# RMSNorm with swish on 16384 rows of 512: units of 8 rows instead of 4

## The chip, the core and the metric

The kernel runs on one core of a Trainium2 chip. A core has several engines that run side by side, each with its own queue of instructions: VectorE (DVE in the profile), ScalarE (ACT), GpSimd (POOL), SyncE (SP, which only issues transfers here) and TensorE (PE, which here only passes semaphores on). Sixteen DMA engines move data between the chip's memory (HBM) and the core's on-chip memory (SBUF). The metric is the device time of one execution in microseconds (us). Less is better.

## The reference

```python
x: (16, 1024, 512) float32, gamma: (512,) of ones, eps = 1e-5
rms = np.sqrt(np.mean(x ** 2, axis=-1, keepdims=True) + eps)
x_norm = x / rms * gamma
return (x_norm * (1.0 / (1.0 + np.exp(-x_norm)))).astype(np.float32)
```

The input is 33.55 MB and so is the output. Each element is read once and written once.

## The kernel before

The 16384 rows are spread over 128 partitions, 128 rows each, and "row" below means one row on each of the 128 partitions (2 KB each, 262 KB in all). A piece (a, n) is the rows a to a+n-1. All work is done in place in a ring `xb` of 96 rows in SBUF, so rows 96 to 127 take the places of rows 0 to 31 once these are stored.

SyncE's queue holds an order written out by hand (`order`). First come the loads of rows 0 to 95 in seven pieces. The queue then waits until (64,28) has landed, issues the stores (0,16) and (16,16), and then the loads (96,16), (112,12) and (124,4); the first of them waits for store (0,16), the second for store (16,16). It waits again until (112,12) has landed and issues the remaining stores (32,32), (64,32), (96,16), (112,8) and (120,8). Each store waits until `s_swish` has counted the units that cover its rows (`ends`). At the end the queue waits for the last stores.

Work goes in units of `cn` = 4 rows, 32 units in all. For unit k:

- `square` (ScalarE, L193 and L199): two rows are squared one at a time, with the hardware summing them into `ms` (each is an activation followed by a read of the accumulator); the two others are squared together into `sq`, which lies in the accumulator memory PSUM.
- `sums` (VectorE, L220): one reduction of `sq` gives the other two columns of `ms`.
- `power` (GpSimd, L175 and L182): adds eps, then raises to the power -0.5, giving `rstd`.
- `norm` (VectorE, L230): each row times its `rstd` times gamma, one instruction a row, in place.
- `swish` (ScalarE, L205): one Silu over the four rows, in place.

The engines are staggered by `lead` = 2 units. ScalarE goes: square of unit k+2, Silu of unit k. VectorE goes: sums of unit k+1, norm of unit k. ScalarE, VectorE and GpSimd each have a hardware loop with `turn` = 3 units per round, ten rounds. `ms`, `rstd` and `sq` have three buffers, one for each unit of a round. The place in the ring is computed in registers: ahead of nearly each instruction stands a register instruction that computes its address. TensorE's queue waits for each load in turn and counts the landed units into `s_land`, for which the squares wait.

Of the kernel before, what the change touches and what calls it, by code (L numbers as in the profile page):

```python
# [9 lines left out]
def kernel(  # L10
# [7 lines left out]
    nc = tc.nc  # L18
    P = nc.NUM_PARTITIONS
    AF = mybir.ActivationFunctionType  # L20
    ALU = mybir.AluOpType
    fp32 = mybir.dt.float32
# [3 lines left out]
    R, D = xf.shape  # L26

    groups = [16, 16, 32, 32, 16, 16]
    ring = 96
    loads = [(0, 4), (4, 4), (8, 8), (16, 16), (32, 32), (64, 28), (92, 4)]  # L30
    second = len(loads)
    loads += [(96, 16), (112, 12), (124, 4)]
    stores = [(0, 16), (16, 16)]
    storing = len(stores)
    stores += [(32, 32), (64, 32), (96, 16), (112, 8), (120, 8)]
    order = [("load", i) for i in range(second)]
    order += [("landed", loads.index((64, 28)))]
    order += [("store", t) for t in range(storing)]
# [1 line left out]
    order += [("landed", loads.index((112, 12)))]  # L40
    order += [("store", t) for t in range(storing, len(stores))]
    early = 2
    cn = 4
    n_sq = 2
    turn = 3
    lead = 2

    first = [sum(groups[:g]) for g in range(len(groups))]
# [9 lines left out]
    K = rows_each // cn  # L58
    assert (K - lead) % turn == 0 and ring % (turn * cn) == 0
    rounds = (K - lead) // turn  # L60
    per_ring = ring // (turn * cn)
# [9 lines left out]
    inv_d = 1.0 / float(D)  # L71
# [5 lines left out]
    def sbuf(name, shape, dt=fp32):  # L77
        return nc.alloc_sbuf_tensor(name, shape, dt).ap()

    xb = sbuf("xb", [P, ring, D])  # L80
    gamma4 = sbuf("gamma4", [P, D])
    gamma_sb = sbuf("gamma_sb", [P, D])
    neg_half = sbuf("neg_half", [P, cn])
# [1 line left out]
    aeps = sbuf("aeps", [P, turn, cn])  # L85
    rstd = sbuf("rstd", [P, turn, cn])
    sq = [nc.alloc_psum_tensor(f"sq{i}", [P, n_sq, D], fp32).ap() for i in range(turn)]
    junk = [nc.alloc_psum_tensor(f"junk{i}", [P, D], fp32).ap() for i in range(2)]
    junk += [sbuf(f"junk{i}", [P, D]) for i in range(2, turn * (cn - n_sq))]

    ld = [nc.alloc_semaphore(f"ld{t}") for t in range(len(loads))]
    st = [nc.alloc_semaphore(f"st{t}") for t in range(len(stores))]
# [2 lines left out]
    s_half = nc.alloc_semaphore("s_half")  # L95
    s_gamma = nc.alloc_semaphore("s_gamma")
    s_land = nc.alloc_semaphore("s_land")
    s_acc = nc.alloc_semaphore("s_acc")
    s_sq = nc.alloc_semaphore("s_sq")
    s_sum = nc.alloc_semaphore("s_sum")  # L100
    s_eps = nc.alloc_semaphore("s_eps")
    s_rstd = nc.alloc_semaphore("s_rstd")
# [3 lines left out]
    def need(ins, sem, value):  # L106
        return ins.wait_op(sem, value, "sem-ge")
# [17 lines left out]
    def load(i):  # L125
        a, n = loads[i]
        for u, (c, m) in enumerate(stores):
            over = c + ring < a + n and a < c + m + ring
            if over and u not in stored_by_sync:
                nc.sync.wait_ge(st[u], 16)  # L130
                stored_by_sync.add(u)
        return nc.sync.dma_start(
            out=buf(loads[i]), in_=dram(xf, loads[i])
        ).then_inc(ld[i], 16)
# [9 lines left out]
    for t in range(early):  # L144
        ins = load(t).ins
        assert here[-1] is ins or here[-1].name == ins.name
        here.pop()
        at = next(
            i for i, other in enumerate(entry)
            if other.engine == mybir.EngineType.SP  # L150
            and isinstance(other, mybir.InstDrain)
        )
# [7 lines left out]
    def take(queue, sem, n):  # L160
        need(queue.nop(nofuse=True), sem, n).then_inc(sem, -n)
# [10 lines left out]
    def power(k, nth):  # L172
        m = k % turn
        need(
            nc.gpsimd.tensor_scalar(  # L175
                out=aeps[:, m, :], in0=ms[:, m, :], scalar1=eps_f, scalar2=None,
                op0=ALU.add,
            ),
            s_sum, nth + 1,
        ).then_inc(s_eps, 1)  # L180
        need(
            nc.gpsimd.tensor_tensor(  # L182
                out=rstd[:, m, :], in0=aeps[:, m, :], in1=neg_half, op=ALU.pow
            ),
            s_eps, nth + 1,
        ).then_inc(s_rstd, 1)

    def rows(at, n):
        return xb[:, at : at + n, :] if isinstance(at, int) else xb[:, bass.ds(at, n), :]

    def square(k, at, sem, count, accs):
        for j in range(n_sq, cn):
            acc = nc.scalar.activation(  # L193
                out=junk[(k % turn) * (cn - n_sq) + j - n_sq], in_=rows(at + j, 1)[:, 0, :], func=AF.Square,
                scale=inv_d**0.5, accum_out=ms[:, k % turn, j : j + 1],
            )
            if j == n_sq:
                need(acc, sem, count)
        nc.scalar.activation(  # L199
            out=sq[k % turn], in_=rows(at, n_sq), func=AF.Square, scale=inv_d**0.5,  # L200
        ).then_inc(s_sq, 1)

    def swish(at, nth):
        need(
            nc.scalar.activation(out=rows(at, cn), in_=rows(at, cn), func=AF.Silu),  # L205
            s_norm, nth + 1,
        ).then_inc(s_swish, 1)
# [5 lines left out]
    nc.scalar.preload_act_table_set("silu_and_others")  # L213
    for k in range(lead):
        assert landings[k] == [k]
        square(k, k * cn, ld[k], 16, k * (cn - n_sq))

    def sums(k, nth):
        need(
            nc.vector.tensor_reduce(  # L220
                out=ms[:, k % turn, 0:n_sq], in_=sq[k % turn], op=ALU.add,
                axis=mybir.AxisListType.X,
            ),
            s_sq, nth + 1,
        ).then_inc(s_sum, 1)

    def norm(k, at, nth):
        for j in range(cn):
            row = rows(at + j, 1)[:, 0, :]
            ins = nc.vector.scalar_tensor_tensor(  # L230
                out=row, in0=row, scalar=rstd[:, k % turn, j : j + 1], in1=gamma_sb,
                op0=ALU.mult, op1=ALU.mult,
            )
            if j == 0:
                need(ins, s_rstd, nth + 1)
        ins.then_inc(s_norm, 1)

    sums(0, 0)
    need(
# [1 line left out]
    ).then_inc(s_gamma, 1)  # L241
    nc.vector.wait_ge(s_gamma, 1)

    with nc.Fori(0, rounds, engines=[mybir.EngineType.Activation]) as i:  # L244
        now = nc.scalar.snap((i % per_ring) * (turn * cn))
        then = nc.scalar.snap(((i + 1) % per_ring) * (turn * cn))
        for m in range(turn):
            behind = now + (m + lead) * cn if m + lead < turn else then + (m + lead - turn) * cn
            square(m + lead, behind, s_land, m + 1, lead * (cn - n_sq) + m * (cn - n_sq))
            swish(now + m * cn, m)  # L250
        take(nc.scalar, s_land, turn)
        take(nc.scalar, s_norm, turn)
    for m in range(lead):
        swish((rounds * turn + m) * cn % ring, m)

    with nc.Fori(0, rounds, engines=[mybir.EngineType.DVE]) as i:
        now = nc.vector.snap((i % per_ring) * (turn * cn))
        for m in range(turn):
            sums(m + 1, m + 1)
            norm(m, now + m * cn, m)  # L260
        take(nc.vector, s_sq, turn)
        take(nc.vector, s_rstd, turn)
    sums(K - 1, 1)
    for m in range(lead):
        norm(rounds * turn + m, (rounds * turn + m) * cn % ring, m)

    with nc.Fori(0, rounds, engines=[mybir.EngineType.Pool]) as i:
        for m in range(turn):
            power(m, m)
        take(nc.gpsimd, s_sum, turn)  # L270
        take(nc.gpsimd, s_eps, turn)
    for m in range(lead):
        power(rounds * turn + m, m)

    for t in range(len(stores)):
        if t not in stored_by_sync:
# [36 lines left out]
```

## Time and profile before

| | |
|---|---|
| time, median of 3 runs (range) | 159.81 us (159.76 to 160.4) |
| profiled execution, its own time | 159.97 us |
| its span, first to last instruction | 158.5 us |
| ScalarE busy | 129.7 us (82% of the span) |
| VectorE busy | 124.5 us (79%) |
| GpSimd busy | 65.4 us (41%) |
| moved | 67.12 MB, 424 GB/s over the span |
| norm, one row of 512 (L230) | 744 ns |
| Silu, 4 rows (L205) | 1903 ns |
| reduction, 2 rows (L220) | 1224 ns |
| square, 2 rows together (L199) | 1005 ns |
| square, 1 row (L193) and the read of its sum | 603 ns and 186 ns |
| add of eps and power, 4 columns (L175, L182) | 643 ns and 1378 ns |

How to read the lines that follow. A page line of groups gives line, engine, operation, output and input, count, busy time and mean length. A line of waits gives who waited for whom, the total, the number of times and the longest. A line of the timeline gives start, length, engine, line and operation; in brackets stands the idle time ahead of it and what ended it. A name with a q (SPq, PEq) is the engine's own queue. The DMA row of the page gives the busy share of the DMA engines in 40 equal slices of the span, in tenths, where 9 is 90% or more.

### The profile page before, as it was taken

How to read it: one execution, taken by the hardware profiler on the slowest of the kernel's cores; microseconds unless marked ns; L12 is line 12 of the kernel's file. 1: busy time of each engine (PE TensorE's matmuls, PEld its weight loads, DVE VectorE, ACT ScalarE, POOL GpSimd, SP SyncE). 2: the span in 40 equal slices, each digit the busy share in tenths (PEclk: the TensorE clock that was granted, in tenths of full speed). 3: DMA queues.
4: the chain of work that ended last, by engine and by line, in shares of the span. 5: the costliest groups of instructions: out<-in, count | busy, mean ns of one | idle time of the engine just before them, and what ended most of it. 6: DMA issues, size and time to landing. Idle time of an engine off the chain costs nothing. (4 is left out here: it accounts for less than half of the span.)

```text
span 158.5 us, 896 instructions
## 1 busy us (share of the span) xinstructions
DVE 124.5 (79%) x162; ACT 129.7 (82%) x193; POOL 65.4 (41%) x70
## 2 busy tenths in 40 slices
DVE  0187968999199999999999999999999999980000
ACT  0949959995599999999999999999999999663000
POOL 1053555555055555555555555555555555500000
DMA  7999997989999969999999999896996996999996
GB/s 256 445 492 397 397 612 314 529 380 414 463 463 463 405 279 440 513 414 397 397 455 463 407 428 529 364 529 281 513 529 265 529 513 281 405 496 414 389 414 265
DMA packets 2456, 67.12 MB, mean 424 GB/s; under 512 B 276, under 2 KB 276, under 8 KB 280
## 3 DMA queue, kind: packets, MB, share of 16 engines
q1 hardware_dynamic: 2448, 67.11, 98.6%
q10 hardware_dynamic: 8, 0.01, 0.0%
HBM read 33.56 MB, written 33.55 MB: 424 GB/s over the span
## 5 line engine op out<-in xcount | busy, mean ns | idle before, releaser
L230 DVE SCALAR_TENSOR_TENSOR xb<-xb,rstd,gamma_sb 128x512 f32 (+1 forms) x128 | 87.3, 744 | 0.0
L205 ACT ACTIVATE xb<-xb (+1 forms) x32 | 60.9, 1903 | 2.8 <-DVE xb L230 2.8
L220 DVE TENSOR_REDUCE ms<-sq 128x2 f32<-128x1024 f32 x32 | 39.2, 1224 | 17.4 <-ACT sq L199 14.2
L175 POOL TENSOR_SCALAR aeps<-ms 128x4 f32<-128x4 f32 x32 | 20.6, 643 | 69.0 <-DVE ms L220 69.0
L182 POOL TENSOR_TENSOR rstd<-aeps,neg_half 128x4 f32<-128x4 f32 x32 | 44.1, 1378 | 2.7
L193 ACT ACTIVATE junk<-xb 128x512 f32 (+1 forms) x64 | 38.6, 603 | 7.7 <-PEq L166 7.5
L199 ACT ACTIVATE sq<-xb 128x1024 f32 (+1 forms) x32 | 32.2, 1005 | 0.0
L193 ACT ACTIVATION_READ_ACCUMULATOR junk<-xb 128x1 f32 x64 | 11.9, 186 | 0.0
L213 ACT ACT_TABLE_LOAD x1 | 1.3, 1283 | 3.6 <-issue 3.6
L168 POOL MEMSET gamma<- 128x512 f32 x1 | 0.5, 524 | 1.5 <-POOLq L75 1.5
L240 DVE STREAM_SHUFFLE gamma_sb<-gamma 128x512 f32<-128x512 f32 x1 | 0.7, 719 | 0.0
L294 POOL MEMSET const-float32-0.0<- 128x1 f32 x1 | 0.1, 98 | 0.2 <-issue 0.2
L294 POOL MEMSET const-uint8-127<- 128x1 uint8 x1 | 0.1, 102 | 0.0
L294 POOL MEMSET const-bfloat16-1.0<- 128x1 bf16 x1 | 0.1, 101 | 0.0
L169 POOL MEMSET neg_half<- 128x4 f32 x1 | 0.1, 101 | 0.0
L294 POOL MEMSET const-float32-1.0<- 128x1 f32 x1 | 0.1, 98 | 0.0
L240 DVE LOAD_MASK_SELECT gamma_sb<-gamma x1 | 0.0, 14 | 0.0
## 6 DMA issues: line engine op xcount, KB each, us to landing
out_dram<-xb SPq DMA_DIRECT2D x3, 4096.0 KB, 19.5
xb<-in_x_dram SPq DMA_DIRECT2D x2, 4096.0 KB, 19.6
xb<-in_x_dram SPq DMA_DIRECT2D x1, 7168.0 KB, 54.8
xb<-in_x_dram SPq DMA_DIRECT2D x4, 1024.0 KB, 13.0
out_dram<-xb SPq DMA_DIRECT2D x2, 2048.0 KB, 15.5
xb<-in_x_dram SPq DMA_DIRECT2D x1, 3072.0 KB, 16.9
xb<-in_x_dram SPq DMA_DIRECT2D x1, 2048.0 KB, 10.2
out_dram<-xb SPq DMA_DIRECT2D x2, 23.9
```

Source lines behind the costliest of these rows:

```text
L168: nc.gpsimd.memset(gamma4, 0.0).then_inc(s_zero, 1)
L169: nc.gpsimd.memset(neg_half, -0.5).then_inc(s_half, 1)
L175: nc.gpsimd.tensor_scalar(out=aeps[:, m, :], in0=ms[:, m, :], scalar1=eps_f, scalar2=None, op0=ALU.add,),
L182: nc.gpsimd.tensor_tensor(out=rstd[:, m, :], in0=aeps[:, m, :], in1=neg_half, op=ALU.pow),
L193: acc = nc.scalar.activation(out=junk[(k % turn) * (cn - n_sq) + j - n_sq], in_=rows(at + j, 1)[:, 0, :], func=AF.Square, scale=inv_d**0.5 ...
L199: nc.scalar.activation(out=sq[k % turn], in_=rows(at, n_sq), func=AF.Square, scale=inv_d**0.5,).then_inc(s_sq, 1)
L205: nc.scalar.activation(out=rows(at, cn), in_=rows(at, cn), func=AF.Silu),
L213: nc.scalar.preload_act_table_set("silu_and_others")
L220: nc.vector.tensor_reduce(out=ms[:, k % turn, 0:n_sq], in_=sq[k % turn], op=ALU.add, axis=mybir.AxisListType.X,),
L230: ins = nc.vector.scalar_tensor_tensor(out=row, in0=row, scalar=rstd[:, k % turn, j : j + 1], in1=gamma_sb, op0=ALU.mult, op1=ALU.mult,)
L240: nc.vector.stream_shuffle(gamma_sb, gamma4, [0] * 32), s_gld, 16
L294: nc = _bacc.Bacc("TRN2", target_bir_lowering=False, num_devices=1)
```

## The change

A unit is 8 rows instead of 4, so there are 16 units, and a round has two of them, seven rounds in all. `lead` stays at two units, now 16 rows. In a unit four rows are squared together and four one at a time, and the joint square now comes first; `s_sq` is counted by the last single row. One reduction makes four columns, and one add and one power make eight. `ms`, `rstd` and `sq` have two buffers instead of three. Since the single rows of unit k+2 then write where unit k's sums stood, they wait for `s_free`, which the first norm of unit k counts.

The addresses of a round are computed together at its head (`addresses`), and the instructions take them from registers. GpSimd's loop is written out as 32 instructions. The two first loads (0,4) and (4,4) become (0,8), and the two last stores (112,8) and (120,8) become (112,16).

```diff
-    loads = [(0, 4), (4, 4), (8, 8), (16, 16), (32, 32), (64, 28), (92, 4)]
+    loads = [(0, 8), (8, 8), (16, 16), (32, 32), (64, 28), (92, 4)]
...
-    stores += [(32, 32), (64, 32), (96, 16), (112, 8), (120, 8)]
+    stores += [(32, 32), (64, 32), (96, 16), (112, 16)]
...
-    cn = 4
-    n_sq = 2
-    turn = 3
+    cn = 8
+    n_sq = 4
+    turn = 2
     lead = 2
...
+    row = D * mybir.dt.size(fp32)
+    xb8 = sbuf("xb", [P, ring * row], mybir.dt.uint8)
+    xb = xb8.bitcast(fp32).rearrange("p (r d) -> p r d", d=D)
...
-    junk = [nc.alloc_psum_tensor(f"junk{i}", [P, D], fp32).ap() for i in range(2)]
-    junk += [sbuf(f"junk{i}", [P, D]) for i in range(2, turn * (cn - n_sq))]
+    junk = [sbuf(f"junk{i}", [P, D]) for i in range(cn - n_sq)]
...
+    def square(k, at, sem, count, free):
+        need(
+            nc.scalar.activation(
+                out=sq[k % turn], in_=rows(at, n_sq), func=AF.Square,
+                scale=inv_d**0.5,
+            ),
+            sem, count,
+        )
         for j in range(n_sq, cn):
             acc = nc.scalar.activation(
...
+            if j == n_sq and free is not None:
+                need(acc, *free)
+        acc.then_inc(s_sq, 1)
...
             if j == 0:
-                need(ins, s_rstd, nth + 1)
+                need(ins, s_rstd, nth + 1).then_inc(s_free, 1)
         ins.then_inc(s_norm, 1)
+
+    def addresses(queue, base, offsets):
+        for c in offsets:
+            nc.lower_val(base + c * row + 16512, [queue])
...
+            ahead = (m + lead) * cn
+            at = (now, ahead) if ahead < span else (then, ahead - span)
+            square(m + lead, at, s_land, m + 1, (s_free, m + 1))
+            swish((now, m * cn), m)
...
-        now = nc.vector.snap((i % per_ring) * (turn * cn))
+        now = nc.vector.snap((i % per_ring) * (span * row))
+        addresses(mybir.EngineType.DVE, now, range(span))
...
-    with nc.Fori(0, rounds, engines=[mybir.EngineType.Pool]) as i:
-        for m in range(turn):
-            power(m, m)
-        take(nc.gpsimd, s_sum, turn)
-        take(nc.gpsimd, s_eps, turn)
-    for m in range(lead):
-        power(rounds * turn + m, m)
+    for k in range(K):
+        power(k, k)
```

## The prediction

> **What bounds the kernel now.** I read the page's DMA rows first, then the waits of the DMA queue, then the timeline of ScalarE and VectorE, then that of the queue's issues.
>
> ```profile
> DMA  7999997989999969999999999896996996999996
> ...
> q1 hardware_dynamic: 2448, 67.11, 98.6%
> ```
>
> The sixteen DMA engines are occupied for 98.6% of the span: 67.11 MB in 158.5 us. No slice stands empty. So the transfers are the bound, and the engines only have to hand over each store in time. The waits of the queue show what it waited for:
>
> ```profile
> SPq L156 <- DMA xb<-in_x_dram: 69.8, 2, 53.7
> SPq L138 <- ACT xb L205: 45.1, 4, 15.6
> SPq L277 <- DMA out_dram<-xb: 14.2, 3, 4.8
> ```
>
> The 45.1 us in which the queue waited for Silu (L205) look like a cost but are not: while it waited, earlier transfers were still moving. The last line gives the landing times: the three last stores land at 148.8, 153.6 and 158.4, that is 4.8 us for each 8-row store. Counting back with 9.8 us for 16 rows (4.19 MB at 428 GB/s), store (64,32) lands at 139.0 and (32,32) at 119.4. Forwards, the loads land at 7.4, 12.2, 21.9, 41.25 and 58.2: 0.606 us a row. Everything is one unbroken pipe, and a store must be in its queue before the pipe runs dry. Here are the issues:
>
> ```profile
> 97.32 16.30 SPq L138 DMA_DIRECT2D out_dram<-xb  x2
> 113.28 0.34 SPq L138 DMA_DIRECT2D out_dram<-xb  x1
> 129.25 8.32 SPq L138 DMA_DIRECT2D out_dram<-xb  x2
> 143.85 0.33 SPq L138 DMA_DIRECT2D out_dram<-xb  x1
> ```
>
> (32,32) is issued at 97.32, (64,32) at 113.28, (96,16) at 129.25, (112,8) at about 137.2, (120,8) at 143.85. What an issue into an empty pipe costs is seen only at the start: 8 rows issued at 0 landed at 7.4, of which 8 x 0.606 = 4.85 is moving, so 2.5 us is fixed. Store (64,32) therefore had to be issued by 119.4 - 2.5 = 116.9; it came at 113.28, 3.6 us early. That margin is what the change acts on.
>
> The compute cycle, from the timeline in mid-kernel (start, us, engine):
>
> ```profile
> 41.29 0.63 ACT L193 ACTIVATE junk<-xb 128x512 f32 x1 [3.28 <-PEq L166]
> ...
> 95.38 1.91 ACT L205 ACTIVATE xb<-xb  x1
> 95.45 1.22 DVE L220 TENSOR_REDUCE ms<-sq 128x2 f32<-128x1024 f32 x1
> 96.59 2.73 DVE L230 SCALAR_TENSOR_TENSOR xb<-xb,rstd,gamma_sb 128x512 f32 x4
> ...
> 97.19 0.61 ACT L193 ACTIVATE junk<-xb 128x512 f32 x1
> ...
> 97.81 0.61 ACT L193 ACTIVATE junk<-xb 128x512 f32 x1
> ...
> 98.42 1.00 ACT L199 ACTIVATE sq<-xb 128x1024 f32 x1
> 99.37 1.90 ACT L205 ACTIVATE xb<-xb  x1
> ```
>
> ScalarE has no gap: Silu 1.81 from start to start, two rows of 0.615, the square of two rows 0.95: 3.99 for 4 rows. VectorE needs 1.14 + 2.83 = 3.97 and keeps in step. The line at 41.29 is ScalarE's last wait for a load, (32,32). From there it runs without a stop, and its pace decides when (64,32) is ready.
>
> **The change part by part.**
>
> *Lag.* `lead` stays 2 but a unit is now 8 rows, so the squares run 16 rows ahead of Silu instead of 8. At 41.29 ScalarE has done Silu on rows 0-15 (before: 0-23) and goes on with the square of unit 4. That is one 8-row Silu more behind the last stall: 3.6 us, on the path to every later store.
>
> *Bigger instructions.* Per 8 rows ScalarE loses one square and one Silu start. From 1024 to 2048 elements the start-to-start time grows by 1.81 - 0.95 = 0.86, so a fixed 0.10 each is saved. New unit: square of 4 rows 0.95 + 0.86 = 1.81, four accumulating rows 4 x 0.615 = 2.46, Silu of 8 rows 1.81 + 2 x 0.86 = 3.53: 7.80, against 2 x 3.99 = 7.98. VectorE: one reduction 1.14 + 1024 elements more (1.22 us hold 1024, less a fixed 0.15, so 1.07) = 2.21, eight norms 7 x 0.662 + 0.744 = 5.38 (the last eight of before took 5.38): 7.59. Its reduction now waits for the last accumulator read, which ends about 0.13 after the next Silu starts, and Silu follows the last norm by 0.04: 7.76. The two still fit, with nothing to spare, and I take 7.80 a unit. Bounds: 7.6 if the fixed part is 0.20 (one square of 512 elements lasts 0.603 and one of 1024 lasts 1.005, so 2 x 0.603 - 1.005), 8.0 if nothing is gained or VectorE's round start shows.
>
> A rule speaks here: the Trainium skill, "VectorE: DVE Perf Modes", in its errata section, says that VectorE and ScalarE pay a fixed extra latency per SBUF instruction, and its ScalarE row (224 cycles at 1.2 GHz) makes that 0.19 us. By it the unit would be 7.98 - 0.37 = 7.61 and the time an estimated 160.8; the trace shows 0.10 from start to start.
>
> *Power.* Sixteen pairs on GpSimd instead of 32. The add of 4 columns took 0.64 mean, the power 1.38; for 8 columns each lies between the same and double, 2.0 to 4.0 a pair. From a reduction's end to the norm that needs it there are 5.4 us of the earlier unit's norms and then another reduction, so this is free to 7 us. The unrolling removes loop instructions that nothing waited for.
>
> *Addresses.* Before: one fused register instruction of 0.07 ahead of every norm, 0.055 ahead of ScalarE's operations. After: three at the head of each of 7 rounds, before the first reduction or square. On ScalarE an 8-row Silu of 3.5 us covers them. On VectorE the last norm, 0.74 us, covers three of 0.07 to 0.14 with the two takes and the branch; uncovered, 0.3 a round, 0.15 a unit, which is inside the bound of 8.0.
>
> *New wait.* The first accumulating row of unit k+2 waits for `s_free`, the first norm of unit k. That norm ends 0.13 + 2.21 + 0.74 = 3.1 us after the Silu before it starts; ScalarE comes there after 3.53 + 1.81 = 5.3. Behind it in ScalarE's queue stand the other three rows and the next Silu, and VectorE's reduction waits for the last row; with 2.2 us in hand none of them is held up. `sq` and `ms` go from three buffers to two under the same cover.
>
> *Loads.* The first 8 rows land at 7.4 as one piece; the first square starts 2.5 us later than before. ScalarE then waits for (8,8) at 12.2 and for (16,16) at 21.9 anyway, so this costs nothing; without that cover, 2.5. Stores (0,16) and (16,16) need units 0-3: the fourth Silu ends at 57.0, and they go out at 58.2. All later loads keep their times.
>
> *Last store.* (112,8) could go at 137.2; (112,16) goes when the last Silu ends.
>
> *Sum.* Unit 4's squares run 41.29 + 4.27 = 45.55, where Silu of unit 2 starts. Silu of unit 11 (row 95) starts 9 x 7.80 later and takes 3.62: 119.4 (before: 113.2). Store (64,32) issues at 119.4 and lands at 119.4 + 2.5 + 32 x 0.6125 = 141.5, against 139.0: a hole of 2.5. (96,16) is ready at 135.0, early enough: 151.3. At the end, Silu of unit 13 starts at 131.35; the reduction ends at 133.7, norms of 14 at 139.0, of 15 at 144.35, Silu to 148.0. (112,16) issues then; 148.0 + 2.5 = 150.5 is under 151.3, so the pipe holds, and it lands at 161.1. The span is 161.1, 2.6 longer. The profiled execution took 159.97, 1.47 more than its span and 0.16 above the median of 159.81. So 161.1 + 1.47 = 162.6.
>
> **The rivals.**
>
> *Fast enough units (no change).* If (64,32) issues by 116.9, the pipe never dries and the span stays 158.5, the time 159.97. That needs (116.85 - 3.62 - 45.55) / 9 = 7.52 a unit or less; 7.61 leaves 0.8 lost (160.8). For it: the fixed part is the least known term, and an issue may enter the pipe in less than 2.5, since about 1.1 of that is landing, seen when the last packets end at 157.3 and the queue's wait at 158.4. Against it: 0.10 a start is what both forms show.
>
> *VectorE's round start, or any hand-over, sets the pace.* At 8.2 a unit, (64,32) issues at 123.0 and the span is 164.7, the time 166.1; above 8.17 the last Silu governs, with 11 units instead of 9. For it: VectorE has 0.04 to spare. Against: before shows no cost at round ends, 3.97 to 4.01 throughout.
>
> *Fewer transfers (faster).* Two transfers fall away. If each paid its own 2.5 even inside a queue, the time would be 159.97 - 5.0 = 155.0. The rows speak against it: the queue's last 8-row stores land 4.8 apart, which 8 x 0.6125 = 4.9 of moving fills.
>
> This is the rule of the Trainium skill, "SBUF — State Buffer", in its section on the DMA setup-cost knee: each transfer pays about 2 us, so coalesce. It would give an estimated 156 here; the trace bears it out only at the start, when the queue is empty.
>
> *The change does not do what it says.* The instruction order on each engine of the changed kernel shows 8-row units, two to a round, and 16 pairs of add and power, so 0.01.
>
> **How the numbers follow.** A hole before (64,32) of 1 to 4.5 us: 0.60, giving 161.0 to 164.5. No hole or one under 0.8: 0.15. A slower pace than 8.0: 0.18, giving 164.5 to 168. Fewer transfers: 0.06. Change absent: 0.01, no change. About 0.8 us, 0.5%, is what a measurement of this kernel can tell from no change. So faster 0.06, same 0.16, slower 0.78. The range of 159.7 to 166.0 leaves out the faster case and the far half of the slow one.
>
> **What would show it.** Right: Silu of 8 rows near 3.6 us, 7.8 from one to the next; the store of rows 64-95 issued near 119.4; a slice near 118 to 121 with the DMA share clearly lower; last store issued near 148. Wrong: that store issued before 117, no dip, and a span of 158.5; or VectorE idle for over 0.3 at each round start and units above 8.0.

## The result, and the profile after

The changed kernel takes 161.34 us (median of 6 runs, 161.15 to 161.43), the one before 159.94 in the same runs: 1.0077 times as long, interval 1.0062 to 1.0092. It is slower by 0.8%, in the direction that was forecast and by about half of the size: 1.4 us instead of 2.6. The profiled execution took 161.26, with a span of 159.3. So the span grew by 0.8 and what lies around it by 0.5, from 1.47 to 1.96.

The two DMA rows of the page after, as they were shown of before:

```profile
DMA  7999996997999969999999999699669969899996
...
q1 hardware_dynamic: 2160, 67.11, 98.2%
```

The share times the span gives 156.4 us of moving, and 156.3 before: the packets took as long as they had, and the 0.8 is time in which nothing moved. Where, the slices cannot tell, since a 6 stands in several places of both rows.

Then the issues of the stores, from the timeline of the queue's engine:

```profile
97.39 0.34 SPq L139 DMA_DIRECT2D out_dram<-xb  x1
119.01 0.34 SPq L139 DMA_DIRECT2D out_dram<-xb  x1
134.53 0.33 SPq L139 DMA_DIRECT2D out_dram<-xb  x1
147.59 0.33 SPq L139 DMA_DIRECT2D out_dram<-xb  x1
```

Store (64,32) left at 119.01 (forecast 119.4, before 113.28), (96,16) at 134.53 and the last at 147.59 (forecast 148.0). What that did to the transfers shows in one stretch of the trace, before and after (the stretch, its length, busy time of VectorE, ScalarE and GpSimd, clock, DMA share, GB/s):

```profile
116.60:119.60 3.00, 2.90 (x6) 3.00 (x7) 2.04 (x2) 1.00 0.81 350
...
116.60:119.60 3.00, 3.00 (x4) 3.00 (x2) 1.63 (x2) 1.00 0.00 0
```

Around here the trace records the packets of the stores in bursts of 1.05 MB, 2.4 us apart, so that a stretch of 3 us holds one burst (350 GB/s) or two. After, this stretch holds none: that is the hole. The records run ahead of the landings (that of (32,32) is at 119.3), so it stands somewhat before the 118 to 121 that were forecast. From 118 to 121 itself the trace shows 655 GB/s before and 350 after, but a stretch without a hole can show 350 too (before, 115 to 118).

The waits of the queue give the end:

```profile
SPq L139 <- ACT xb L219: 49.1, 3, 21.3
...
SPq L303 <- DMA out_dram<-xb: 11.3, 2, 9.6
```

The last two waits end at 149.6 and 159.2: the last store moves its 16 rows in 9.6, right behind the one ahead of it. Before, the store of rows 96-111 landed at 148.7. So all that the span lost was lost before this store had landed, and nothing behind it.

The unit, from the timeline:

```profile
107.62 3.60 ACT L219 ACTIVATE xb<-xb  x1
107.75 2.29 DVE L236 TENSOR_REDUCE ms<-sq 128x4 f32<-128x2048 f32 x1 [0.17 <-ACT junk L209]
109.96 5.38 DVE L246 SCALAR_TENSOR_TENSOR xb<-xb,rstd,gamma_sb 128x512 f32 x8
...
111.13 1.86 ACT L202 ACTIVATE sq<-xb 128x2048 f32 x1
112.93 0.61 ACT L209 ACTIVATE junk<-xb 128x512 f32 x1
...
115.38 3.60 ACT L219 ACTIVATE xb<-xb  x1
```

From Silu to Silu 7.76 (forecast 7.80). VectorE waits 0.17 in each unit for the last accumulator read and ends its norms at 115.34, 0.04 ahead of the Silu that needs them: the two fit with nothing to spare, as was worked out.

### The profile page after: what moved, and what is told of

Same layout as the page of the kernel before. It is cut to its first block, busy times and chain, and to the rows that moved or that the text cites. A ratio compares the mean times of both kernels' runs of the same rounds, so it can differ in the third digit from the quotient of the medians.

```text
span 159.3 us, 525 instructions
## 1 busy us (share of the span) xinstructions
DVE 122.1 (77%) x146; ACT 126.1 (79%) x161; POOL 42.8 (27%) x38
## 5 line engine op out<-in xcount | busy, mean ns | idle before, releaser
L246 DVE SCALAR_TENSOR_TENSOR xb<-xb,rstd,gamma_sb 128x512 f32 (+1 forms) x128 | 86.0, 745 | 0.0
L219 ACT ACTIVATE xb<-xb (+1 forms) x16 | 57.7, 3605 | 5.8 <-DVE xb L246 5.8
L236 DVE TENSOR_REDUCE ms<-sq 128x4 f32<-128x2048 f32 x16 | 36.7, 2292 | 21.9 <-ACT junk L209 21.9
L202 ACT ACTIVATE sq<-xb 128x2048 f32 (+1 forms) x16 | 29.9, 1867 | 12.0 <-PEq L167 9.2
L209 ACT ACTIVATE junk<-xb 128x512 f32 (+1 forms) x64 | 39.2, 613 | 0.0
L176 POOL TENSOR_SCALAR aeps<-ms 128x8 f32<-128x8 f32 x16 | 10.3, 642 | 90.3 <-DVE ms L236 90.3
L183 POOL TENSOR_TENSOR rstd<-aeps,neg_half 128x8 f32<-128x8 f32 x16 | 31.7, 1984 | 1.3
```

What stands on the lines that cost most here:

```text
L176: nc.gpsimd.tensor_scalar(out=aeps[:, m, :], in0=ms[:, m, :], scalar1=eps_f, scalar2=None, op0=ALU.add,),
L183: nc.gpsimd.tensor_tensor(out=rstd[:, m, :], in0=aeps[:, m, :], in1=neg_half, op=ALU.pow),
L202: nc.scalar.activation(out=sq[k % turn], in_=rows(at, n_sq), func=AF.Square, scale=inv_d**0.5,),
L209: acc = nc.scalar.activation(out=junk[j - n_sq], in_=rows(down(at, j), 1), func=AF.Square, scale=inv_d**0.5, accum_out=ms[:, k % turn, j : ...
L236: nc.vector.tensor_reduce(out=ms[:, k % turn, 0:n_sq], in_=sq[k % turn], op=ALU.add, axis=mybir.AxisListType.X,),
L246: ins = nc.vector.scalar_tensor_tensor(out=one, in0=one, scalar=rstd[:, k % turn, j : j + 1], in1=gamma_sb, op0=ALU.mult, op1=ALU.mult,)
```

## The experiments

Two questions were open: is the late store all that the span lost, and what is the price of a late issue; and where do the 0.5 around the span come from. All ran beside the kernel before; "around" is the time less the span, median over each kernel's runs.

| kernel | time | ratio to before, interval | span | around |
|---|---|---|---|---|
| before | 160.0 | | 158.5 | 1.50 |
| changed | 161.34 | 1.0077 (1.0062 to 1.0092) | 159.35 | 1.97 |
| changed, store cut | 160.83 | 1.0046 (1.0033 to 1.0058) | 158.9 | 1.99 |
| changed, GpSimd loop back | 161.35 | 1.0072 (1.0051 to 1.0093) | 159.4 | 1.92 |
| before, GpSimd written out | 159.98 | 0.9997 (0.9983 to 1.0011) | 158.5 | 1.51 |
| before, late store | 163.07 | 1.0182 (1.0158 to 1.0205) | 161.6 | 1.52 |
| before, first load 8 rows | 159.99 | 1.0000 (0.9991 to 1.0009) | 158.5 | 1.50 |
| before, last store 16 rows | 160.11 | 1.0005 (0.9996 to 1.0014) | 158.6 | 1.51 |
| changed, both stores cut | 160.08 | 1.0003 (0.9991 to 1.0014) | 158.2 | 1.85 |
| changed, load cut | 160.02 | 1.0005 (0.9987 to 1.0024) | 158.1 | 2.00 |
| the same, own addresses | 160.61 | 1.0027 (1.0008 to 1.0046) | 159.3 | 1.34 |
| changed code, units of 4 | 159.53 | 0.9969 (0.9950 to 0.9988) | 158.2 | 1.31 |
| load cut, two programs padded | 159.74 | 0.9981 (0.9972 to 0.9990) | 158.4 | 1.32 |
| load cut, VectorE padded | 159.69 | 0.9980 (0.9971 to 0.9989) | 158.4 | 1.34 |

### The store of rows 64 to 95 cut in two

```diff
-    stores += [(32, 32), (64, 32), (96, 16), (112, 16)]
+    stores += [(32, 32), (64, 16), (80, 16), (96, 16), (112, 16)]
```

> The changed kernel with store (64,32) cut into (64,16) and (80,16), so that its first half waits for 10 units of Silu instead of 12. In the changed kernel unit 9's Silu ends at 103.5, so the first half would be in the queue 15 us before the pipe could run dry. Theory 'hole': the span was 0.8 longer because (64,32) came at 119.0 into an empty pipe; then the span goes back to 158.5 and the second half, at 119.0, is covered. With the 1.96 around the span that the changed kernel showed, the time is 160.4. Rival 'pace of the transfers' (the bigger first and last pieces or a slower mix of loads and stores cost the 0.8): the span stays 159.3, the time 161.3.

The span went to 158.9, not to 158.5. Why half a way only is in its own trace, in the queue's waits and its last issue:

```profile
SPq L303 <- DMA out_dram<-xb: 10.6, 2, 10.4
...
147.87 0.33 SPq L139 DMA_DIRECT2D out_dram<-xb  x1
```

The wait for the last store is now 10.4, where it was 9.6. The first hole is closed, the stores ahead land 1.2 earlier than in the changed kernel, at 148.4 (147.87, the issue of 0.33 and the other wait of 0.2), and now the last one, issued at 147.87, comes too late: a second hole had stood behind the first, covered by it. Neither theory had that.

### The price of a late issue by itself

```diff
-            s_swish, ends[t],
+            s_swish, ends[t] + (2 if stores[t] == (64, 32) else 0),
```

> The kernel before with store (64,32) held back for two more units of Silu (26 instead of 24), so that it is issued at 121.25 instead of 113.28; nothing else is moved. It prices a late issue by itself. The prediction's own term (an issue lands 2.5 later than moving alone, deadline 116.9) gives a hole of 4.4: span 162.9, time 164.3. By the result, where an issue at 119.0 cost 0.8, the deadline is 118.2 and the hole 3.0: span 161.5, time 163.0. By the rival 'pace of the transfers' the late issue is hidden and the span stays within 0.5 of 158.5.

Nothing but one issue is moved here, from 113.28 to 121.28:

```profile
121.28 8.32 SPq L138 DMA_DIRECT2D out_dram<-xb  x2
```

The span is 161.6, 3.1 longer. Set beside the changed kernel: an issue 2.27 later (121.28 less 119.01) and a span 2.25 longer (161.6 less 159.35). Between these two runs each microsecond of delay costs one, and counted back by it the deadline is 121.28 - 3.1 = 118.2. Store (32,32) lands at 119.4, so an issue into a pipe that runs dry lands its rows 119.4 - 118.2 = 1.2 later than moving alone takes, not 2.5. The expectation that was worked out from the result (161.5) held, the one from the prediction's term (162.9) did not.

The price can also be read without the span. The trace gives the time from the issue of (64,32) to its landing, here for the kernel before, the changed one and this run:

```profile
out_dram<-xb SPq DMA_DIRECT2D x1, 25.7
...
out_dram<-xb SPq DMA_DIRECT2D x1, 20.8
...
out_dram<-xb SPq DMA_DIRECT2D x1, 20.8
```

Before, the store lands at 113.28 + 25.7 = 139.0, having waited behind (32,32). In the two late runs it takes the same 20.8, though the issues are 2.27 apart. At the 0.6125 a row of the sum, 32 rows move in 19.6, which leaves 1.2. At 0.60 a row, as the changed kernel's last store moved (9.6 for 16 rows), it is 1.6. So the price is 1.2 at the pace that the sum uses, and at most about 1.6.

### Both stores cut, and the load cut instead

```diff
-    stores += [(32, 32), (64, 32), (96, 16), (112, 16)]
+    stores += [(32, 32), (64, 16), (80, 16), (96, 16), (112, 8), (120, 8)]
```

> The changed kernel with store (64,32) cut into (64,16) and (80,16) and the last store cut into (112,8) and (120,8), as before had the last two. With the first cut alone the span was 158.9: store (112,16) came at 147.9, while the store ahead of it landed at 148.5 and an issue into a pipe that runs dry costs about 1.25 more than its moving, so there was a second hole of 0.6. Theory 'two holes in a row': (112,8) goes at about 142.5 and covers (120,8) at 147.9; the second hole closes and the span is 158.5. Rival 'uneven drain or pace': 158.9 stays. For the 0.5 around the span: 160.0 if the last store carries it, 160.5 if not.

The span is 158.2: with a piece of the last store ready at 142.4, the second hole is closed too.

```diff
-    loads = [(0, 8), (8, 8), (16, 16), (32, 32), (64, 28), (92, 4)]
+    loads = [(0, 8), (8, 8), (16, 16), (32, 16), (48, 16), (64, 28), (92, 4)]
```

> The changed kernel with load (32,32) cut into (32,16) and (48,16). ScalarE then need not wait until 41.3 for unit 4 but goes on at 37.5, when Silu of unit 1 ends, and keeps 3.7 all the way. Store (64,32) is issued at 115.3, the last at 143.9. Theory 'lag': the late hand-over came from the 16 rows of lead at the last stall; both holes close, with no store cut, and the span is 158.5, the time 160.0 to 160.5 by what lies around it. Rival 'pace of the transfers': span stays 159.3.

Here no store is touched; ScalarE only loses its wait for load (32,32) and hands everything over 3.7 earlier:

```profile
115.31 0.34 SPq L139 DMA_DIRECT2D out_dram<-xb  x1
130.83 0.33 SPq L139 DMA_DIRECT2D out_dram<-xb  x1
143.89 0.33 SPq L139 DMA_DIRECT2D out_dram<-xb  x1
```

The issues came to 0.1 where they were expected, and the span is 158.1. So the lag at the last stall made the late stores, and the late stores made all that the span lost; the rival, a slower pace of the transfers, is out. Both runs end 0.3 to 0.4 below the span of before, which was not expected and is not explained; against them, instead of against before, the changed kernel lost 1.2 and not 0.8.

### The 0.5 around the span

```diff
-    nc.scalar.wait_ge(s_sum, 1)
+    nc.scalar.wait_ge(s_free, 1)
...
-    for k in range(K):
-        power(k, k)
+    with nc.Fori(0, rounds, engines=[mybir.EngineType.Pool]) as i:
+        for m in range(turn):
+            power(m, m)
+        take(nc.gpsimd, s_sum, turn)
+        take(nc.gpsimd, s_eps, turn)
+    for m in range(lead):
+        power(rounds * turn + m, m)
```

> The changed kernel with GpSimd's loop put back (two units a round, as before had three) instead of 32 instructions written out; ScalarE's wait ahead of its loop is then on s_free instead of s_sum. Between the time and the span lie 1.96 in the changed kernel and 1.47 in the one before. Theory 'outside, from the longer program': the unrolled GpSimd makes the 0.5; then span 159.3 and time 160.8. Rival 'outside, from something else' (transfers, the other loops): time 161.3 and no change of span.

The same edit turned round, in the kernel before:

> The kernel before with GpSimd's loop alone written out (64 instructions instead of a loop). Theory 'outside, from the longer program': span 158.5, time 0.5 or more longer, 160.5 to 160.9. Rival: nothing changes, 159.9, since no one waits for GpSimd's loop instructions.

1.92 and 1.51: writing out GpSimd's loop costs nothing and gains nothing, in the span or around it. The two transfers that were joined, each alone in the kernel before:

```diff
-    loads = [(0, 4), (4, 4), (8, 8), (16, 16), (32, 32), (64, 28), (92, 4)]
+    loads = [(0, 8), (8, 8), (16, 16), (32, 32), (64, 28), (92, 4)]
...
-        assert landings[k] == [k]
-        square(k, k * cn, ld[k], 16, k * (cn - n_sq))
+        square(k, k * cn, ld[0], 16, k * (cn - n_sq))
```

> The kernel before with the two first loads (0,4) and (4,4) as one, (0,8); both first units wait for it. Between the time and the span lie 1.50 before and 1.98 after, and GpSimd's loop was not the reason. Theory 'first load': the 0.5 comes with the bigger first transfer, then span 158.5 and time 160.5. Rival 'last store' or 'something in the loops': nothing changes, span 158.5, time 160.0.

```diff
-    stores += [(32, 32), (64, 32), (96, 16), (112, 8), (120, 8)]
+    stores += [(32, 32), (64, 32), (96, 16), (112, 16)]
```

> The kernel before with the two last stores (112,8) and (120,8) as one, (112,16), which is issued at 143.9 as (120,8) was. The store before it lands at 148.7, so the pipe does not run dry. Theory 'last store': the 0.5 around the span comes with the bigger last transfer, then span 158.5 and time 160.5. Rival 'first load' or 'something in the loops': span 158.5, time 160.0. If big last pieces drain unevenly, the span itself grows by some tenths.

1.50 and 1.51, with ratios of 1.0000 and 1.0005: neither is it, and neither is worth anything in time. That left the loops of ScalarE and VectorE. First the grouping of the addresses was taken away from the kernel with the cut load:

```diff
-        addresses(mybir.EngineType.Activation, now, [m * cn for m in range(turn)])
-        for m in range(lead, lead + turn):
-            at = (now, m * cn) if m < turn else (then, m * cn - span)
-            addresses(
-                mybir.EngineType.Activation, at[0],
-                [at[1] + j for j in [0, *range(n_sq, cn)]],
-            )
...
-        addresses(mybir.EngineType.DVE, now, range(span))
```

> The changed kernel with load (32,32) cut in two, as in the run that closed both holes (span 158.1, time 160.0, 1.98 around the span), and with the addresses no longer computed together at the head of a round: each instruction has its own register instruction ahead of it again, as before had. Theory 'grouped addresses': the 0.5 around the span comes with them; then about 1.5 around a span of 158.1 and a time of 159.6, the fastest so far. Rival 'units of 8 or the other edits': 1.98 stays, time 160.1. If the register instructions between norms cost VectorE time, the issues come later than 115.3 and 143.9, up to the point where a hole opens again (about 118.1).

Around the span it fell to 1.34, but the span rose to 159.3, and scattered: 158.6 to 159.8 over the 12 runs. The stores of the late part went out at 115.33 and 143.91, so the register instructions cost VectorE nothing; in the profiled run (span 159.6) the loads ran late (store (32,32), which waits for a load, left at 98.83 instead of 97.35), and why is not known. Next the changed code at before's sizes:

```diff
-    cn = 8
-    n_sq = 4
-    turn = 2
+    cn = 4
+    n_sq = 2
+    turn = 3
```

with before's loads and stores.

> The changed kernel's code (grouped addresses, s_free, joint square first, GpSimd written out) at before's sizes: units of 4 rows, three to a round, and before's loads and stores. Theory 'grouped addresses': 1.98 around the span, time 160.5 at a span of 158.5. Rival 'units of 8': 1.5 around the span, time 160.0. For the lag: with units of 4 the lead is 8 rows again and store (64,32) should go near 113.3 to 114, without a hole, so the span is 158.5; the lag, not the code, made the late store.

1.31, so the grouped addresses do not make the 0.5 either. This kernel has the shortest time of all, 0.3% under before, interval 0.1% to 0.5%; the two padded kernels below, at 0.2%, lie within that interval. Its store (64,32) left at 113.52, so the code without the bigger units leaves the margin whole. So the theory of grouped addresses falls, and units of 8 are not it by themselves either, since the run before this one had them and 1.34. What both have in common is programs of another length. The last pair, on the kernel with the cut load, changes the length alone:

```diff
+    for _ in range(26):
+        nc.vector.wait_ge(s_gamma, 1)
+    for _ in range(18):
+        nc.scalar.wait_ge(s_gld, 16)
```

> The changed kernel with load (32,32) cut in two (span 158.1, 2.00 around it, time 160.0), and at the end of VectorE's and ScalarE's programs 26 and 18 waits on semaphores that have long been reached, so that both programs are as long as in the run with own addresses (68 and 52 instructions), which had 1.34 around its span of 159.3. The waits run while the last stores are still moving, so nothing waits for them. Theory 'what lies around the span hangs on how long or how placed the programs are': about 1.34 around a span of 158.1, time 159.5, faster than both kernels. Rival 'it hangs on what the instructions do (grouped addresses together with units of 8)': 2.00 stays and the time is 160.0. Whether the span also rises, as it did to 159.3 there, shows if that too came with the length.

The same without the two last lines:

> The same with the 26 waits on VectorE alone. Theory 'length or place of the programs': a value between 1.3 and 2.0 that tells which engine's program counts (1.34 if VectorE's does, 2.00 if ScalarE's). Rival 'what the instructions do': 2.00, time 160.0.

1.32 and 1.34 instead of 2.00 (that was on another chip, but the kernel before had 1.51 there and 1.50 here). Waits that are reached long ago, at the end of VectorE's program alone, take 0.66 off the time around the span; half of that comes back in it (158.4 instead of 158.1). So that part hangs on how long VectorE's program is, or on how the programs come to lie. A row appears on the page that the unpadded kernel lacks:

```profile
q14 instruction: 1, 0.01, 0.0%
```

It is a transfer of instructions within the span, and four of the five kernels with such a row had 1.31 to 1.34 around it; the fifth, before with GpSimd written out, had 1.51, as before without the row. So the row by itself does not set the time around the span. That the loading of programs is behind it is a guess that was not tested, and the cause of the 0.5 stays open.

## Why the prediction was half right

**What bounds the kernel, and the place of the loss: right.** The transfers are the bound, store (64,32) was late, and a hole stood before it. The runs with the cut load and the cut stores closed it and got the whole of the span back.

**Lag and pace: right.** Unit 4 began at 41.28, Silu of unit 2 at 45.54, a unit took 7.76, the store left at 119.0 for 119.4. The joint instructions save 2 x 3.99 - 7.76 = 0.22 a unit, 0.11 for each start saved, against 0.10 forecast. The Trainium skill ("VectorE: DVE Perf Modes", errata) would have made it 0.37. By the length of a Silu the trace agrees with its 0.19 (2 x 1.903 - 3.605 = 0.20), by that of the joint square less so (2 x 1.005 - 1.867 = 0.14). But the sum needs the time from start to start, and there less is saved, because an instruction starts before the one ahead has ended: the Silu of eight rows lasts 3.60, and the next instruction starts 3.51 after it.

One reading in the prediction's part on the lag is short: it prices the eight rows at 3.6, one Silu. Their squares stand in the path too, 80 rows behind the stall instead of 72, and the sum, which counts unit by unit, has both. Measured, the store left 5.73 later (119.01 less 113.28): eight rows at the old pace, 8.0, less ten units at 0.22.

**The price of an issue into an empty pipe: wrong, and the step that failed.** The sum took 2.5 from the only row that it had, the first load of the kernel. In mid-kernel it is 1.2 by the same pace of 0.6125 a row, shown twice, in the changed kernel and in the run with one late store: both stores landed 20.8 after their issue. That is 1.3 of the 1.75 by which the span was over-forecast; the remaining 0.4 is 9 units at 0.04 each. With both put right the sum is 119.0 + 1.2 + 19.6 + 9.8 + 9.8 = 159.4, and 159.35 was measured. The text had seen that 1.1 of the 2.5 might not count, since it is landing, and used it only for a rival. 2.5 - 1.1 = 1.4 is near what was measured; that the landing of the store ahead runs beside the start of the next one is argued from this, not shown. The Trainium skill ("SBUF — State Buffer", the setup-cost knee) gives about 2 us a transfer; no run here shows that in mid-kernel.

**What lies around the span: wrong, though smaller.** The sum carried it over as 1.47, without a reason why the change should leave it alone, and it came out as 1.97. So the two errors have opposite signs: the span came out 1.75 shorter than forecast and the rest 0.5 longer, and the forecast of 2.6 became 1.4. That the time is closer to its forecast than the span is luck.

**The last store: right, for the reason given.** The sum said that (112,16) at 148.0 would be covered by a pipe that was late already, and so it was: 147.59 + 1.2 = 148.8, and the store ahead landed at 149.6. What it did not say is that this holds only while the first hole stands. With that one closed the last store was not covered, as the first run showed.

**Power, addresses, new wait, first load: right.** The power of 8 columns took 1.98, and nobody waited for it; ScalarE shows no wait for `s_free`; joining the first loads is worth nothing, and so is joining the last stores. That settles the rival of fewer transfers: neither pair paid a price inside the queue that joining saves.

**Units fast enough for no change** did not come about, but it was nearer than it looked: with the deadline at 118.2 instead of 116.9, units of 7.67 would by the same sum have been enough.

## What to carry to other kernels

Where transfers are the bound, find for each store the time by which it must be in the queue, and judge every change of the compute by those times alone: bigger units made ScalarE and VectorE quicker here and the kernel slower, since a lead counted in units grew with them. The price of a missed deadline should come from a row in mid-kernel, and where there is none, be given both ends, not the start-up's. And when a hole is closed, look for the next one behind it.

## What was not expected of the hardware

An issue into a pipe that has run dry cost 1.2 us beyond its moving in mid-kernel (1.6 by the faster pace), where the first load of the kernel paid 2.5. The one is a store and the other a load; no run separates that from the place in the kernel. The time around the span, the same to 0.25 us in nearly all the runs of one kernel, went from 1.31 to 2.00 between kernels, and 26 waits that held nothing up at the end of one engine's program moved it by 0.66.
